# Adding the partial sums of the FFNs' second product into y by an accumulating DMA instead of VectorE

## The chip, the cores and the metric

The kernel runs on one core of a Trainium2 chip. The core has five engines that run side by side, each through its own list of instructions in order: TensorE (PE, matrix products, with its weight loads shown apart as PEld), VectorE (DVE), ScalarE (ACT), GpSimd (POOL) and SyncE (SP, which in this kernel only issues transfers). Matrix products land in PSUM; everything else works in SBUF. The metric is the device time of one execution in microseconds; lower is better.

## The reference, cut to what matters

Two layers of a sequence model over 512 latent and 256 context tokens, each a mixer followed by a SwiGLU FFN of width 2816 on 1024 features. Layer 0's FFN runs on all 768 tokens, layer 1's on the 512 latent ones. The change is inside these two FFNs:

```python
def _swiglu(h, w_gate, w_up, w_down):
    return (jax.nn.silu(h @ w_gate) * (h @ w_up)) @ w_down
...
for l in range(DEPTH):
    ...                                                   # mixer of layer l, out-projection, norms
    h_lat = _modulate(_rms(x_lat, norm_pre_ffn[l]), m_lat[3], m_lat[4])
    x_lat = x_lat + m_lat[5] * _rms(_swiglu(h_lat, ffn_w_gate[l], ffn_w_up[l], ffn_w_down[l]), norm_post_ffn[l])
```

The first product is the pair `h @ w_gate`, `h @ w_up`; the second product is the one with `w_down`. Its sum over the 2816 inner columns is what `y` collects.

## The kernel before, in words

**Numbers.** Every float32 matrix operand is split into a rounded part H and a rest L, and a product is three matmuls (H·H, H·L, L·H). So each weight tile that arrives by DMA (`raw`, 128x1024, a ring of three buffers) is cast by ACT (`wH`, L686 and L741) and subtracted by DVE (`wL`, L687 and L742) before PE can use it. A `raw` buffer comes free when its last cast and subtraction are done, and only then SP, which issues the weight loads in a fixed order, can issue the load that goes into it. L686/L687 are the rows of `w_down`; L741/L742 and the sums `ws`, `raw` (L766) belong to `w_gate` and `w_up`.

**The FFN loop** (function `ffn`) walks the 22 column blocks of 128 two at a time (`c0`). The first two blocks come early (`pearly`). From then on each turn does three things:

- a gate product `go` and an up product `uo`, each by a seven-product scheme on 2x2 blocks (function `seven`; its products have the names 11, U1, 12, U2, 22, S4, V in this order). Product 11, U2 and V use one half of a PSUM tile `ab`, product 12 the other half; E and D are two single PSUM banks. ACT and DVE move each result from PSUM into `go` or `uo`: ACT copies 11 (L805), U1 (L807), U2 (L815), 22 (L817); DVE adds 12 (L813), S4 (L820) and V (L822, L823).
- DVE multiplies `uo` by `go` (L1520); ACT and DVE split the result into `gH`, `gL` (L1522, L1523). `go` and `uo` have one buffer each.
- the second product for the previous pair of blocks (function `acc_part`): for every token tile of 128, PE sums 2 blocks x 3 matmuls for each half of 512 output columns in PSUM (`acc`), and the sum is then added to `y` in SBUF. The tiles take turns in PSUM: one tile takes the two-bank tile `mm` and is added as one 128x1024 piece (a whole), the next takes the two single banks that E and D also use and is added as two 128x512 pieces (halves). The first turn of each layer writes `y` by an ACT copy (L832). All later turns add by DVE (L834). In the last call two blocks are summed together, and each tile goes on to the final norm.

There are ten turns of the loop in each layer; the second product is run for nine of them inside the loop and once after it. Layer 0 has six token tiles, layer 1 four. During layer 0's FFN the kernel also computes modulation vectors in DVE's gaps: DMA loads `mraw`, DVE sums (`macc`, L542, L544).

The program text does not fix the order on each engine. A scheduler arranges all instructions with a cost model of its own, so an edit at one place moves instructions at others. Within an engine the order is then fixed, and an instruction that waits holds all behind it.

Of the kernel before, what the change touches and what calls it, by code (L numbers as in the profile page):

```python
# [8 lines left out]
F32 = mybir.dt.float32  # L9
# [4 lines left out]
ALU = mybir.AluOpType  # L14
# [3 lines left out]
P = 128  # L18
D = 1024
# [311 lines left out]
class Net:  # L331
# [490 lines left out]
                nc.vector.tensor_tensor(c21, c21, pt, op=ALU.subtract)  # L822
                nc.vector.scalar_tensor_tensor(c22, pt, -1.0, c22, op0=ALU.mult, op1=ALU.subtract)  # L823

    def acc_part(self, parts, n, tiles, groups, ys, first, end):


        nc = self.nc

        def add(y, pt):  # L830
            if first:
                nc.scalar.copy(y, pt)  # L832
            else:
                nc.vector.tensor_tensor(y, y, pt, op=ALU.add)  # L834

        for group in groups:
            pts = {}
            for i in group:

                self.whole = not self.whole  # L840
                pt = self.mm_tile("acc") if self.whole else None
                pts[i] = pt, [pt[:, :512], pt[:, 512:]] if self.whole else [self.sc_tile("acc", x) for x in range(2)]
            for p, (units, act) in enumerate(parts):
                done = p == len(parts) - 1
                for i in group:
                    whole, halves = pts[i]
                    t = tiles[i]
                    H, L = (x[:, :, i * P % n : i * P % n + P] for x in act[i * P // n])
                    for hf in range(2):
                        cs = slice(hf * 512, hf * 512 + 512)  # L850
                        for c, unit in enumerate(units):
                            self.mm3(
                                halves[hf],
                                (H[:, c, :], L[:, c, :]),
                                (unit[0][:, 0, cs], unit[1][:, 0, cs]),
                                p == 0 and c == 0,
                                done and c == len(units) - 1,
                            )
                        if done and hf == 0:
                            self.turn(1)  # L860
                        if done and whole is None:
                            add(ys[:, t, cs], halves[hf])
                    if done:
                        if whole is not None:
                            add(ys[:, t, :], whole)
                        end(ys[:, t, :], t)
# [634 lines left out]
    def ffn(self, l, xp, yp, fp, pp, rp, h, ending, extra=None):  # L1501


        nc, I = self.nc, self.I
        wg, wu, wd = I["ffn_w_gate"][l], I["ffn_w_up"][l], I["ffn_w_down"][l]
        tiles, n = h.order, h.n
        extra = extra(fp) if extra else iter(())
        fill = lambda *_: next(extra, None)
        singles = [(i,) for i in range(len(tiles))]

        gp = rp if l else fp

        def gu(x):
            return fp.tile([P, 2, 2 * n], F32, tag=x, bufs=1, name=x)

        def gated(pool, k, g, u, HL=None, mult=True):

            g, u = (x[:, :, n * k : n * k + n] for x in (g, u))
            if mult:
                nc.vector.tensor_tensor(u, u, g, op=ALU.mult)  # L1520
            H, L = HL or h.gated_tiles(pool, k)
            nc.scalar.copy(H, u)  # L1522
            nc.vector.tensor_tensor(L, u, H.bitcast(F32), op=ALU.subtract)  # L1523
            return H, L

        def first():

            cur = h.gated if l else [h.gated_tiles(gp, k) for k in range(2)]
            g, u = gu("go"), gu("uo")
            us = [[self.unit_cols(w, i * P) for w in (wg, wu)] for i in range(2)]  # L1530
            h.open(xp)
            for half in range(2):
                pm = self.mm_tile("pearly")
                pts = [[self.sc_tile("pearly", x)[:, :n] for x in range(2)], [pm[:, 512 * x : 512 * x + n] for x in range(2)]]
                tok = slice(n * half, n * half + n)
                for ks in ((range(4), range(4, 8)) if half == 0 else (range(8),)):
                    for i in range(2):
                        for m in range(2):
                            for k in ks:
                                self.mm3(pts[i][m], tuple(x[:, k, :] for x in us[i][m]), h.raw(k, half), k == 0, k == KD - 1)  # L1540
                            if ks[0] == 0 and half == 0 and m == 0:
                                self.turn(1 - i)
                for i in range(2):
                    nc.scalar.activation(g[:, i, tok], pts[i][0], AF.Silu)
                    nc.vector.tensor_tensor(u[:, i, tok], g[:, i, tok], pts[i][1], op=ALU.mult)
                gated(gp, half, g, u, cur[half], False)
                if half == 0:
                    pp.release()
                    tp = self.open_pool(f"t{l}")
                    h.sums(tp)  # L1550
            h.late()
            return tp, cur

        def units(c0):
            return [self.rows_unit(wd, c0 + i) for i in range(2)]

        def product(w, c0, x, then=None):
            x = gu(x)
            self.seven(self.pair_operands(tp, w, c0 * P, [tp] if l else [], 1 + l), h, x, fill if c0 > 2 else lambda: None, then)
            return x  # L1560

        tp, cur = first()
        y = None
        todo = None
        for c0 in range(2, NFC, 2):
            g = product(wg, c0, "go", todo)
            for k in range(2):
                x = g[:, :, n * k : n * k + n]
                nc.scalar.activation(x, x, AF.Silu)
            if c0 + 2 < NFC:  # L1570
                if y is None:
                    y = yp.tile([P, len(tiles), D], F32, tag="y", bufs=1, name=f"y{l}")
                self.acc_part([(units(c0 - 2), cur)], n, tiles, singles, y, c0 == 2, fill)
                u = product(wu, c0, "uo")
                cur = [h.gated_tiles(gp, k) for k in range(2)]

                def todo(g=g, u=u, cur=cur):
                    for k in range(2):
                        gated(gp, k, g, u, cur[k], True)

            else:
                u = product(wu, c0, "uo")
        for _ in extra:
            pass
        tp.release()
        if gp is not rp:
            rp.release()
        end, follow, pool = ending(y)

        last = [gated(pool, k, g, u) for k in range(2)]  # L1590
        parts = [(units(c0 - 2), cur), (units(c0), last)]
        next(follow, None)
        self.acc_part(parts, n, tiles, [(0, 1)] + singles[2:], y, False, end)
        for left in (2, 1, 0):
            next(follow, None)
            self.turn(left)
        next(follow, None)
        if gp is rp:
            rp.release()
        return y  # L1600
# [232 lines left out]
```

## Time and profile before

| quantity | value |
|---|---|
| time, median of 3 runs | 1762.86 us (1760.73, 1762.86, 1765.64) |
| span of the profiled execution, first to last instruction | 1764.6 us |
| own time of the profiled execution | not given apart from its span |
| mean granted TensorE clock in it | 0.993 |
| PE, DVE, ACT, POOL busy | 1713.0, 1268.5, 865.9, 74.2 us |
| layer 0's FFN loop, steady part | about 480 to 920 us of the span |
| layer 1's FFN loop, steady part | about 1420 to 1740 us of the span |

The span of the profiled execution lies inside the spread of the runs, 1.7 us above their median. In the rows of the profile an instruction group reads: line of the kernel, engine, operation, output and inputs by the program's names, shapes, count, busy time, mean duration in ns, and after the bar the engine's idle time just before these instructions and what ended it. In a list of waits the three numbers are total time, number of waits, and the longest one.

### The profile page before, as it was taken

Reading aid. Unit: us, or ns where it says so; the run is one execution under the profiler, and the core shown is the slowest. Engines: PE = TensorE matmul, PEld = TensorE weight load, DVE = VectorE, ACT = ScalarE, POOL = GpSimd, SP = SyncE. Lnnn points to the kernel's source line nnn. Section 1 sums busy time; section 2 is a strip of 40 time slices with the busy share of each in tenths; the row PEclk is TensorE's granted clock in tenths of the full one; section 3 lists DMA queues with packets and bytes.
Section 4 is the critical chain, followed back from the end, with each engine's and each line's share of the span. In section 5 each row is a group of like instructions: output and inputs, shape, how many; then the busy total and the mean of one; then the engine's idle time right before and its main releaser. Section 6 shows DMA issues by size and latency. Waiting matters only on the chain. (4 is left out here: it accounts for less than half of the span.)

```text
span 1764.6 us, 33117 instructions
## 1 busy us (share of the span) xinstructions
PE 1713.0 (97%) x13888; PEld 1559.9 (88%) x13888; DVE 1268.5 (72%) x2008; ACT 865.9 (49%) x1496; POOL 74.2 (4%) x93
## 2 busy tenths in 40 slices
PE   6999999999999999999999999999999999999998
PEld 3899998988998989889998998888898889998997
DVE  5879646644968999797667418787764678878885
ACT  5545557736543233333346526666654654444343
POOL 1004100001000000000001000000000100000000
PEclk8999999999999999999999999999999999999999
DMA  8731011143434455352225322121124333333333
GB/s 316 225 105 39 2 61 62 49 144 115 136 102 124 146 172 186 113 197 72 72 72 170 104 61 61 50 61 49 50 62 131 120 96 96 96 97 107 98 103 123
DMA packets 169585, 187.26 MB, mean 106 GB/s; under 512 B 6198, under 2 KB 140892, under 8 KB 169436
## 3 DMA queue, kind: packets, MB, share of 16 engines
q1 hardware_dynamic: 167504, 181.56, 32.6%
q10 hardware_dynamic: 1932, 3.59, 0.6%
q8 instruction: 109, 1.79, 0.4%
q14 instruction: 40, 0.33, 0.1%
HBM read 175.66 MB, written 9.46 MB: 105 GB/s over the span
## 5 line engine op out<-in xcount | busy, mean ns | idle before, releaser
L687 DVE TENSOR_TENSOR wL<-raw,wH 128x1024 fp32r<-128x1024 f32 (+1 forms) x126 | 151.2, 1206 | 116.7 <-ACT wH L686 116.4
L362 PE MATMUL nat<-wH,x 128*128 128x256 f32 (+1 forms) x1216 | 227.6, 286 | 0.0
L741 ACT CAST wH<-raw 128x1024 fp32r<-128x1024 f32 x120 | 124.6, 1052 | 176.6 <-PE acc L362 73.4
L362 PEld LDWEIGHTS nat<-wH,x 128*128 128x128 f32 x1216 | 192.4, 192 | 2.3 <-ACT natq L1098 0.8
L742 DVE TENSOR_TENSOR wL<-raw,wH 128x1024 fp32r<-128x1024 f32 x120 | 145.2, 1220 | 64.3 <-ACT wH L741 64.2
L686 ACT CAST wH<-raw 128x1024 fp32r<-128x1024 f32 (+1 forms) x126 | 128.9, 1038 | 116.6 <-PE nat L362 34.2
L362 PE MATMUL nat<-wL,x 128*128 128x256 f32 (+1 forms) x608 | 173.0, 285 | 0.0
L362 PE MATMUL acc<-wH,gH 128*128 128x512 f32 x440 | 172.6, 393 | 0.0
L362 PE MATMUL acc<-wH,gL 128*128 128x512 f32 x440 | 171.7, 390 | 0.0
L362 PE MATMUL acc<-wL,gH 128*128 128x512 f32 x440 | 171.5, 390 | 0.0
L834 DVE TENSOR_TENSOR y<-y,acc 128x1024 f32<-128x1024 f32 x135 | 114.8, 862 | 31.3 <-PE acc L362 28.0
L362 PE MATMUL ff<-x,wH 128*128 128x512 f32 (+1 forms) x512 | 127.6, 340 | 0.0
L544 DVE SCALAR_TENSOR_TENSOR macc<-mraw,scT,macc 128x1024 f32<-128x1024 f32 x98 | 122.6, 1276 | 6.3 <-DMA mraw<-in_mod_w_dram 6.3
L614 POOL TENSOR_TENSOR rs<-ms,neghalf 128x1 f32<-128x1 f32 (+2 forms) x62 | 58.2, 939 | 1612.6 <-DVE ms L612 1606.4
L362 PEld LDWEIGHTS nat<-wL,x 128*128 128x128 f32 x608 | 116.9, 192 | 0.1
L362 PE MATMUL oproj<-wH,x 128*128 128x512 f32 x320 | 102.0, 396 | 3.4 <-ACT x L1248 3.4
L362 PEld LDWEIGHTS acc<-wH,gH 128*128 128x128 f32 x440 | 82.6, 188 | 19.7 <-issue 1.7
L362 PEld LDWEIGHTS acc<-wH,gL 128*128 128x128 f32 x440 | 82.6, 188 | 17.3
L362 PEld LDWEIGHTS acc<-wL,gH 128*128 128x128 f32 x440 | 82.7, 188 | 16.2
L362 PEld LDWEIGHTS ff<-x,wH 128*128 128x128 f32 x512 | 87.3, 190 | 10.0
L937 ACT COPY qkh<-arr 128x512 f32<-128x512 f32 x112 | 70.2, 643 | 36.6 <-DVE arr L942 32.4
L362 PE MATMUL ff<-x,wL 128*128 128x256 f32 (+1 forms) x256 | 86.2, 337 | 0.0
(345 smaller groups left out, 4102.9 us busy)
## 6 DMA issues: line engine op xcount, KB each, us to landing
mraw<-in_mod_w_dram SPq DMA_DIRECT2D x96, 512.0 KB, 4.7
raw<-in_ffn_w_gate_dram SPq DMA_DIRECT2D x44, 512.0 KB, 3.8
raw<-in_ffn_w_up_dram SPq DMA_DIRECT2D x44, 512.0 KB, 4.0
raw<-in_ffn_w_down_dram SPq DMA_DIRECT2D x44, 512.0 KB, 3.6
raw<-in_odd_w_in_dram SPq DMA_DIRECT2D x40, 512.0 KB, 4.0
raw<-in_even_w_in_dram SPq DMA_DIRECT2D x16, 512.0 KB, 4.2
x<-xr SPq DMA_DIRECT2D x14, 512.0 KB, 2.7
xr<-x SPq DMA_DIRECT2D x14, 512.0 KB, 3.4
```

The lines of the kernel that those rows point to most:

```text
L362: return self.pin(self.nc.tensor.matmul(*a, **k))
L544: nc.vector.scalar_tensor_tensor(a, u, w, a, op0=ALU.mult, op1=ALU.add)
L614: nc.gpsimd.tensor_tensor(rs, ms, self.neghalf.to_broadcast([P, w]), op=ALU.pow)
L686: nc.scalar.copy(H[:, :m], raw[:, :m])
L687: nc.vector.tensor_tensor(L[:, :m], raw[:, :m], H[:, :m].bitcast(F32), op=ALU.subtract)
L741: self.nc.scalar.copy(H, f)
L742: self.nc.vector.tensor_tensor(L, f, H.bitcast(F32), op=ALU.subtract)
L834: nc.vector.tensor_tensor(y, y, pt, op=ALU.add)
L937: nc.scalar.copy(qkv[:, :, :, half, :], dst)
```

## The change: what it does

`acc_part` gets a function `by_dma`. Where that function gives a buffer (`ypart`), ACT copies the partial sum from PSUM to the buffer, and a DMA issued on POOL's queue adds the buffer to `y` in SBUF. In layer 1 every partial sum of the loop after the first turn goes this way, wholes and halves, with four buffers; in layer 0 only the halves do, with two buffers, and the wholes stay with DVE. The last call, after the loop, stays with DVE in both layers.

```diff
-    def acc_part(self, parts, n, tiles, groups, ys, first, end):
+    def acc_part(self, parts, n, tiles, groups, ys, first, end, by_dma=None):
         nc = self.nc
         def add(y, pt):
             if first:
                 nc.scalar.copy(y, pt)
+            elif by_dma is not None and (s := by_dma(pt.shape[-1])) is not None:
+                nc.scalar.copy(s, pt)
+                nc.gpsimd.dma_start(out=y, in_=s, accum_op=ALU.add)
             else:
                 nc.vector.tensor_tensor(y, y, pt, op=ALU.add)
...
+        def part(m):
+            if l:
+                return fp.tile([P, D], F32, tag="ypart", bufs=4, name="ypart")[:, :m]
+            return fp.tile([P, m], F32, tag="ypart", bufs=2, name="ypart") if m == 512 else None
...
-                self.acc_part([(units(c0 - 2), cur)], n, tiles, singles, y, c0 == 2, fill)
+                self.acc_part([(units(c0 - 2), cur)], n, tiles, singles, y, c0 == 2, fill, part)
```

Line numbers from the inserted lines on shift by 3, and behind `part` by 8 (L1520 becomes L1528, L1523 becomes L1531, L1569 becomes L1577).

The scheduler's new order differs at three places of each turn of layer 1. First ACT, from the Silu of `go` (L1569, now L1577) over the second product to the first copy of the next up product. Before:

```order
L1569 ACTIVATE go<-go 128x2x256 x2
L741 CAST dH<-ws 128x512
L741 CAST wH<-raw 128x1024 x2
L805 COPY uo<-ab 128x256
L807 COPY uo<-E 128x256
```

Now:

```order
L1577 ACTIVATE go<-go 128x2x256 x2
L834 COPY ypart<-acc 128x1024
L741 CAST dH<-ws 128x512
L834 COPY ypart<-acc 128x512 x2
L834 COPY ypart<-acc 128x1024
L834 COPY ypart<-acc 128x512
L741 CAST wH<-raw 128x1024
L834 COPY ypart<-acc 128x512
L741 CAST wH<-raw 128x1024
L805 COPY uo<-ab 128x256
```

Of the two casts that stood together, the second now stands behind the copy of the last half.

Second PE, at the start of the gate product that follows (E is product U1, D is product 22, `ab<-x` is product 12). Before:

```order
L362 MATMUL E<-T_14925,wH 128x256 x2
L362 MATMUL E<-T_14925,wL 128x256
L362 MATMUL D<-x_14765,wH 128x256 x2
L362 MATMUL ab<-x_14764,wH 128x256 x2
L362 MATMUL ab<-x_14764,wL 128x256
```

Now:

```order
L362 MATMUL E<-T_15021,wH 128x256 x2
L362 MATMUL E<-T_15021,wL 128x256
L362 MATMUL ab<-x_14860,wH 128x256 x2
L362 MATMUL ab<-x_14860,wL 128x256
L362 MATMUL ab<-x_14860,wH 128x256 x2
```

Two matmuls of product 22 that stood ahead of product 12 now stand behind it.

Third DVE, from the end of the up product into the gate product (`ws` is the first sum on a newly loaded pair of up weights). Before:

```order
L687 TENSOR_TENSOR wL<-raw,wH 128x1024
L822 TENSOR_TENSOR uo<-uo,ab 128x256
L823 SCALAR_TENSOR_TENSOR uo<-ab,uo 128x256
L1520 TENSOR_TENSOR uo<-uo,go 128x2x256 x2
L687 TENSOR_TENSOR wL<-raw,wH 128x1024
L1523 TENSOR_TENSOR gL<-uo,gH 128x512 x2
L813 TENSOR_TENSOR go<-go,ab 128x256
L766 TENSOR_TENSOR ws<-raw 128x512
```

Now:

```order
L687 TENSOR_TENSOR wL<-raw,wH 128x1024
L822 TENSOR_TENSOR uo<-uo,ab 128x256
L823 SCALAR_TENSOR_TENSOR uo<-ab,uo 128x256
L1528 TENSOR_TENSOR uo<-uo,go 128x2x256 x2
L687 TENSOR_TENSOR wL<-raw,wH 128x1024
L766 TENSOR_TENSOR ws<-raw 128x512
L1531 TENSOR_TENSOR gL<-uo,gH 128x512 x2
L813 TENSOR_TENSOR go<-go,ab 128x256
```

`ws` has moved ahead of the split (L1523, now L1531) and of the addition of product 12 (L813).

## The prediction

> **What bounds the kernel now.** First the busy shares, over the span and over the steady part of each FFN (columns there: stretch, its length, then busy time and count of PE, PEld, DVE, ACT, POOL, granted clock, share of the DMA engines, GB/s).
>
> ```profile
> span 1764.6 us, 33117 instructions
> ...
> PE 1713.0 (97%) x13888; PEld 1559.9 (88%) x13888; DVE 1268.5 (72%) x2008; ACT 865.9 (49%) x1496; POOL 74.2 (4%) x93
> ```
>
> ```profile
> 480.00:920.00 440.00, 433.16 (x2275) 395.80 (x2274) 360.74 (x449) 155.01 (x215) 0.00 (x0) 1.00 0.41 127
> 1420.00:1740.00 320.00, 312.98 (x2159) 290.60 (x2159) 250.13 (x351) 146.22 (x228) 0.00 (x0) 1.00 0.34 103
> ```
>
> PE is the bound: in layer 0's FFN it lacks 6.8 us of 440, in layer 1's 7.0 of 320. So freeing DVE can give back some 14 us at the most, and only where DVE's lateness is what PE waits for. POOL is empty in both, so its queue delays no older work. Next PE's waits, layer 0 (480 to 920) and then layer 1 (1420 to 1740):
>
> ```profile
> PE ab L362 <- DVE uo L813: 3.9, 3, 2.1
> PE ab L362 <- ACT go L805: 1.9, 2, 1.4
> ...
> PE ab L362 <- DVE go L813: 1.0, 2, 0.6
> ```
>
> ```profile
> PE ab L362 <- ACT go L805: 5.0, 9, 1.2
> ```
>
> None is a wait for `acc`'s PSUM to be emptied by the additions (L834). In layer 1 one wait comes back in every turn: product 12 of the gate product waits for ACT's copy of product 11 (L805). The chain of work that ended last shows what makes that copy late (start, length, what):
>
> ```profile
> 1563.70 10.92 PE acc L362 x48
> ...
> 1574.64 0.69 DVE y L834
> 1575.33 2.28 DVE wL L742 x2
> ...
> 1577.63 5.20 DMA raw<-in_ffn_w_up_dram
> ...
> 1582.85 1.06 ACT wH L741
> ...
> 1585.49 1.14 DVE wL L687
> ...
> 1587.80 0.70 DVE uo L1520
> ...
> 1589.03 1.69 PE ab L362 x12
> 1590.72 1.08 PE D L362 x9
> ```
>
> When `acc` ends, DVE adds the last half, makes two `wL`, and with the second a `raw` buffer comes free. Only then can SP issue the next up load. ACT's cast and DVE's `wL` wait for it, and in DVE's order the additions to `uo` and the multiplication L1520 stand behind this `wL`; L1520 frees `go`, ACT copies, PE goes on:
>
> ```profile
> 1583.93 1.23 DVE L742 TENSOR_TENSOR wL<-raw,wH 128x1024 fp32r<-128x1024 f32 x1 [4.48 <-ACT wH L741]
> 1589.03 0.50 PE L362 MATMUL ab<-x,wH 128*128 128x256 f32 x2 [0.98 <-ACT go L805]
> ```
>
> So the 32 us turn already has no slack on this path: whatever delays that load delays PE by as much.
>
> **What the change removes.** The additions by DVE, in layer 0 and in layer 1:
>
> ```profile
> L834 DVE TENSOR_TENSOR y<-y,acc 128x512 f32<-128x512 f32 x48 | 32.5, 683 | 5.8 <-PE acc L362 4.3
> ```
>
> ```profile
> L834 DVE TENSOR_TENSOR y<-y,acc 128x512 f32<-128x512 f32 x32 | 21.9, 686 | 5.6 <-PE acc L362 3.9
> L834 DVE TENSOR_TENSOR y<-y,acc 128x1024 f32<-128x1024 f32 x16 | 19.5, 1217 | 0.2 <-PE acc L362 0.2
> ```
>
> That is 32.5 + 21.9 + 19.5 = 74 us of DVE. In layer 1 it is worth nothing directly: in the chain only the last half (0.69 us) is on the path, and something else takes its place (below). In layer 0 it is worth part of PE's 6.8 us. But the two largest of those waits stand behind a load of modulation weights, not behind additions; DVE idled for it just ahead of L813:
>
> ```profile
> 652.61 1.28 DVE L544 SCALAR_TENSOR_TENSOR macc<-mraw,scT,macc 128x1024 f32<-128x1024 f32 x1 [1.78 <-DMA mraw<-in_mod_w_dram]
> ```
>
> ```profile
> 753.10 1.28 DVE L544 SCALAR_TENSOR_TENSOR macc<-mraw,scT,macc 128x1024 f32<-128x1024 f32 x1 [2.30 <-DMA mraw<-in_mod_w_dram]
> ```
>
> Less DVE work does not bring these loads forward. I leave out about half of the 6.8, and set against the remaining 3.4 some 1.4 for new traffic beside the `mraw` loads: layer 0 gives **-2**, with bounds -6.8 (every wait gone) and +4.1 (DVE's two waits here, 1.78 + 2.30, once more).
>
> **What it adds on ACT.** 80 halves and 16 wholes, priced by the copies of the first turn, which read the same PSUM tile (minimum, median, maximum in ns; the maximum is a whole):
>
> ```profile
> L832 ACT COPY y<-acc x15: 578/591/1018, 489.8 to 1446.4; 128x512 f32<-128x512 f32 x10, 128x1024 f32<-128x1024 f32 x5
> ```
>
> 80 x 0.59 + 16 x 1.02 = 63.5 us. ACT is 35% to 46% busy in the two stretches, so the sum is hidden; the order is not. In layer 1 the last half and the two casts behind `acc` now go copy, cast, copy, cast, with the tile ends read from the chain's 48 matmuls (0.2275 us each): the fifth partial sum is ready at 1573.3 and copied by 1573.9, the first cast runs 1574.0 to 1575.05, the last copy (its sum ready at 1574.6) to 1575.65, the second cast to 1576.65. Before, the casts ended at 1576.01:
>
> ```profile
> 1574.01 2.00 ACT L741 CAST wH<-raw 128x1024 fp32r<-128x1024 f32 x2 [4.16 <-PE acc L362]
> ```
>
> DVE's second `wL` then ends at about 1576.65 + 1.2 = 1577.85 in place of 1577.61: the load is issued **0.25 us later**. Removing DVE's last addition buys nothing, since ACT's copy stands in its place.
>
> **What the new order moves.** PE: two matmuls of 0.12 us (nine took 1.08) that filled time ahead of the wait now stand behind it: **+0.24 us**. DVE: `ws` now stands ahead of L1523 and L813, and needs the second up load.
>
> ```profile
> 1577.63 9.40 SPq L763 DMA_DIRECT2D raw<-in_ffn_w_up_dram  x2
> ```
>
> ```profile
> 1588.40 1.22 DVE L687 TENSOR_TENSOR wL<-raw,wH 128x1024 fp32r<-128x1024 f32 x1
> ...
> 1591.01 0.41 DVE L813 TENSOR_TENSOR go<-go,ab 128x256 f32<-128x256 f32 x1
> ```
>
> ```profile
> raw<-in_ffn_w_gate_dram SPq DMA_DIRECT2D x18, 512.0 KB, 3.7
> raw<-in_ffn_w_up_dram SPq DMA_DIRECT2D x20, 512.0 KB, 4.0
> ```
>
> The second load is issued at about 1586.7 (0.38 us before the row's end) and lands 3.7 us later, at 1590.4 (the median of its neighbour, since the up median of 4.0 includes the crowded first one). `ws` (0.69) ends at 1591.1, L1523 (two, 1.2) at 1592.3, L813 at 1592.7. PE, with products 12, 22 and three matmuls of S4 in between (27 x 0.12 = 3.24 from 1589.03), is ready for U2 at 1592.3: **+0.35 us**. Together the order costs 0.25 + 0.24 + 0.35 = 0.84 us in each of the eight turns that add by DMA; below, these could overlap with each other and cost 0.25.
>
> **What it adds on the queues.** POOL issues 48 + 32 halves (256 KB) and 16 wholes (512 KB), 29 MB, 2.1 MB in each turn of layer 1. No trace shows an accumulating transfer or one issued on POOL, so it is bounded. The nearest row is the weight queue in layer 1 (packets, MB, share of 16 engines):
>
> ```profile
> q1 hardware_dynamic: 42832, 31.99, 33.5%
> ```
>
> 33.5% of 320 us for 32 MB is 3.35 us of all engines per MB. In front of and beside the critical load stand the last three partial sums (a whole copied by 1573.0, halves by 1573.9 and 1575.65), 1.05 MB: 3.5 us if the bytes move once, 7 if reading `y` counts as well. SP's two loads there (a `w_down` load and the critical one) also take 3.5 us. Lower bound of the delay: 0, if the sums have drained first. Upper bound: 3.5 us, if the two queues share the engines evenly all the while. I take **1.5**, near the 1.76 us of the two halves moved once, as the whole is likely gone by 1577.6. [...]
>
> Waits that the buffers add: layer 1's fifth copy (1573.3) needs the first sum (copied by 1567.5) landed, 5.8 us; layer 0's third half needs the first, two tiles or 24 matmuls later: 5.46 - 0.59 = 4.9 us. Against loads of 3.7 to 4.0 us this costs nothing; it comes back as a rival. An addition into the same piece of `y` is a turn of 32 us away, and the tail's additions stay with DVE: nothing there.
>
> **Sum.** Layer 1: 8 x (0.84 + 1.5) = +18.7. Layer 0: -2. Against the profiled span of 1764.6 this gives 1781.3; that span stands 1.7 above the median of the runs, so I forecast **1779**, slower by 0.9%.
>
> **The rivals.**
> - The transfers are hidden: the sums drain before the critical load, and the delay is 0. Then 8 x 0.84 = 6.7, layer 0 -3.4: 1766, no measurable change. For it: the DMA engines are busy only 34% of the time. Against: the load goes out within 2 us of the last copy.
> - Faster: DVE's relief in layer 0 takes away all of PE's 6.8 us, as its `mraw` sums are done sooner, the loads go out sooner and L813 is no longer late: 1756. It decides if layer 1 loses less than 1.5 us in all, that is if the load is no later than now. For it: DVE at 82% is layer 0's busiest helper. Against: the two rows on `mraw` above.
> - Much slower: an accumulating transfer of 512 KB takes longer than 5.8 us. Then ACT waits at its fifth copy with the casts behind it. At 9 us: 3.2 for the buffer, 3.5 for shared engines, 0.84: 7.5 x 8 = 60, so 1823. Against: it needs more than double a load's time. [...]
>
> **How the numbers follow.** Forecast 0.50, hidden 0.22, faster 0.15, much slower 0.13. Two runs of this kernel differ by about 0.3% (5.3 us), so that is what counts as no change. Faster takes the third case, 0.15; same the second with a little of the forecast's low edge, 0.23; slower 0.62. The forecast's own range is 1765 (delay 0.3, overlapped order costs: 8 x 0.55 - 2 = 2.4) to 1802 (delay 3.5, layer 0 at its upper bound: 8 x 4.34 + 4.1 = 38.8). The range of 1757 to 1803 adds the hidden case and nearly all the way to the faster one, and leaves out the much slower one and half of the faster.
>
> **What would show it.** In layer 1 the up load behind `acc` lands more than 5.2 us after its issue, PE's waits on L805 grow from 5.0 us to about 20, L813 of `go` appears among PE's waits, and turns lengthen from 32 to some 34.5 us. In layer 0 PE's waits stay above 3 us. ACT gains 64 us, DVE loses 74. Wrong it is if the load lands as now (then 1766 or less), or if ACT's idle time names POOL's transfers (then well above 1803).

## The result: slower by 2.8%, and the profile after

The changed kernel takes 1811.4 us (median of 4 runs, 1810.1 to 1816.9) against 1764.0 us (4 runs, 1760.7 to 1765.6). The ratio is 1.0281 with a 95% interval of 1.0264 to 1.0298. I had forecast 1779 us with a range of 1757 to 1803: the direction was right, the size was not. The loss is 47.5 us where the sum had 16.7.

First, lines of the page after: span, busy time, DMA queues (packets, MB, share of 16 engines). In the new kernel's numbering the copies stand in L834, the new DMAs in L835, VectorE's remaining additions in L837, and what was L1520, L1523 and L1569 is now L1528, L1531 and L1577.

```profile
span 1810.9 us, 33344 instructions
...
PE 1731.2 (96%) x13888; PEld 1574.0 (87%) x13888; DVE 1203.9 (66%) x1912; ACT 923.7 (51%) x1592; POOL 157.4 (9%) x189
...
q1 hardware_dynamic: 167504, 181.56, 31.7%
q0 software_dynamic: 13824, 29.37, 9.8%
```

ACT has 58 us more and DVE 65 us less, much as announced (the rows of neighbouring instructions overlap by some 0.1 us, so 74 us of rows are 65 of busy time). PE does the same 13888 matmuls in 18 us more, so some of them ran slower. The new queue q0 moved 29.37 MB in 9.8% of the engines' time: 0.098 x 1810.9 / 29.37 = **6.0 us of all engines per MB**, where the weight queue q1 has 0.317 x 1810.9 / 181.56 = 3.2. These shares add up the times of packets (the pieces a transfer is cut into), so "engine time" here means packet time; where packets overlap, the share of a short stretch passes 1 (1.05 below, that is 16.8 packets at once on the mean).

The two FFN stretches after (length, busy time and count of PE, PEld, DVE, ACT, POOL, granted clock, DMA share, GB/s):

```profile
480.00:920.00 440.00, 428.80 (x2234) 390.12 (x2233) 329.33 (x394) 176.89 (x255) 41.91 (x48) 0.99 0.58 153
1420.00:1740.00 320.00, 293.80 (x1925) 271.40 (x1925) 196.19 (x277) 162.40 (x251) 38.46 (x45) 0.95 0.58 136
```

In layer 1 PE now lacks 26 us of 320 (7.0 before), and its granted clock fell from 1.00 to 0.95. The waits there (1425 to 1760; total, times, longest) after:

```profile
ACT wH L741 <- DMA raw<-in_ffn_w_up_dram: 30.4, 9, 5.6
...
PE E L362 <- DVE uo L820: 17.1, 8, 3.5
...
PE ab L362 <- ACT go L805: 9.3, 7, 1.8
...
ACT ypart L834 <- DMA y<-ypart: 0.3, 1, 0.3
```

The first row was 7.3 us in 9 waits in the same window of before. The second is new. It is the same path as in the prediction, met one step earlier: the gate product's second product, U1, writes bank E, and DVE must empty E first (L820). L820 stands in DVE's queue behind the `wL` that waits for the late up load. One turn of the chain of waits after:

```profile
1704.70 0.58 ACT ypart L834
1705.28 0.96 ACT wH L741
...
1706.27 1.24 DVE wL L742
1707.52 9.44 DMA raw<-in_ffn_w_up_dram
...
1716.98 1.05 ACT wH L741
...
1719.20 0.41 DVE uo L820
...
1722.70 0.38 ACT go L805
...
1723.13 2.93 PE ab L362 x12
```

The load takes 9.4 us where the same step took 5.2. The last row shows a second cost: 12 matmuls in 2.93 us, 1.69 before. They come behind PE's longest wait there (the timeline's row of the first U1 product, its wait in brackets):

```profile
1719.67 0.80 PE L362 MATMUL E<-T,wH 128*128 128x256 f32 x2 [3.52 <-DVE uo L820]
```

Why the load is late can be read in the stretches around its issue, and why the matmuls are slow in the stretch after the stall. First before, the 6 us from the load's issue; then after, the 7 us ahead of the issue at 1707.5 (`acc` ends at 1704.4), the 6 us from it, and 6 us after the stall (columns as above):

```profile
1577.00:1583.00 6.00, 6.00 (x50) 5.81 (x50) 1.02 (x2) 0.90 (x3) 0.00 (x0) 1.00 0.64 179
```

```profile
1700.00:1707.00 7.00, 7.00 (x44) 6.26 (x43) 1.96 (x2) 4.35 (x6) 3.32 (x4) 1.00 1.05 189
```

```profile
1707.00:1713.00 6.00, 6.00 (x51) 5.81 (x50) 0.91 (x2) 0.75 (x2) 0.00 (x0) 1.00 1.03 211
```

```profile
1723.00:1729.00 6.00, 5.87 (x27) 5.88 (x28) 4.78 (x8) 2.35 (x7) 0.00 (x0) 0.50 0.45 132
```

The 16 DMA engines are full (1.03; 0.64 before) when the critical load is issued, and they already were in the 7 us ahead of it (1.05). After the stall PE's granted clock is 0.50. The transfers themselves (KB each, median us from issue to landing):

```profile
y<-ypart POOLq DMA_DIRECT2D x80, 256.0 KB, 5.4
...
y<-ypart POOLq DMA_DIRECT2D x16, 512.0 KB, 5.2
```

In layer 0 (480 to 920) the waits after are these; the `macc` row was 6.3 us in 6 waits before, and PE's 3.9:

```profile
ACT ypart L834 <- DMA y<-ypart: 21.4, 8, 7.1
DVE macc L544 <- DMA mraw<-in_mod_w_dram: 18.0, 16, 2.7
PE ab L362 <- DVE uo L813: 6.9, 4, 2.1
```

Where the 46.3 us between the two profiled spans (1764.6 and 1810.9) went, from the starts of the first and last `acc` of each layer in the trace: layer 0 446.0 to 453.2 us (+7.2); between the layers +0.2; layer 1 301.9 to 338.7 (+36.9); before the first `acc` -0.4, behind the last +2.5.

### The profile page after: what moved, and what is told of

Its sections match the earlier page's. It is cut to its first block, busy times and chain, and to the rows that moved or that the text cites. A ratio compares the mean times of both kernels' runs of the same rounds, so it can differ in the third digit from the quotient of the medians.

```text
span 1810.9 us, 33344 instructions
## 1 busy us (share of the span) xinstructions
PE 1731.2 (96%) x13888; PEld 1574.0 (87%) x13888; DVE 1203.9 (66%) x1912; ACT 923.7 (51%) x1592; POOL 157.4 (9%) x189
## 3 DMA queue, kind: packets, MB, share of 16 engines
q1 hardware_dynamic: 167504, 181.56, 31.7%
q0 software_dynamic: 13824, 29.37, 9.8%
## 5 line engine op out<-in xcount | busy, mean ns | idle before, releaser
L687 DVE TENSOR_TENSOR wL<-raw,wH 128x1024 fp32r<-128x1024 f32 (+1 forms) x126 | 151.1, 1205 | 117.3 <-ACT wH L686 116.9
L835 POOL DMA_DIRECT2D y<-ypart x96 | 83.3, 875 | 704.7 <-ACT ypart L834 610.4
L834 ACT COPY ypart<-acc 128x512 f32<-128x512 f32 (+1 forms) x96 | 63.1, 658 | 124.3 <-PE acc L362 100.2
L362 PE MATMUL E<-T,wH 128*128 128x384 f32 (+1 forms) x320 | 73.8, 320 | 17.5 <-DVE uo L820 17.1
```

The source lines that it names most:

```text
L362: return self.pin(self.nc.tensor.matmul(*a, **k))
L687: nc.vector.tensor_tensor(L[:, :m], raw[:, :m], H[:, :m].bitcast(F32), op=ALU.subtract)
L834: nc.scalar.copy(s, pt)
L835: nc.gpsimd.dma_start(out=y, in_=s, accum_op=ALU.add)
```

## The experiments

Theory: the accumulating transfers cost about twice a load's engine time per byte (6.0 against 3.2 us per MB); those in flight when the up load behind `acc` is issued delay it; PE stalls, and restarts at a lower clock (0.50 in the stretch above). Rivals: the new order of instructions (ACT's copies between the casts) costs it, not the transfers; every transfer costs a fixed price; ACT waits for its `ypart` buffers; bytes cost the same wherever they stand in the turn.

All experiments are edits of the changed kernel. "Turn" is the mean time between `acc` starts over turns two to eight of layer 1 in the profiled run, "load" the range of the up loads behind `acc` that the chain shows in those turns, "layer 0" the time from its first to its last `acc`. Each ratio is to runs of the kernel before on the same chip (medians of 1760.9 to 1764.0 us).

| kernel | median us | ratio to before (95%) | turn | load | layer 0 |
|---|---|---|---|---|---|
| before | 1764.0 | | 32.4 | 4.4 to 5.5 | 446.0 |
| changed | 1811.4 | 1.0281 (1.0264 to 1.0298) | 37.3 | 6.8 to 9.4 | 453.2 |
| layer 1 alone | 1801.3 | 1.0227 (1.0210 to 1.0244) | 36.8 | 6.8 to 8.9 | 442.1 |
| layer 0 alone | 1771.1 | 1.0047 (1.0026 to 1.0068) | 32.4 | 4.6 to 5.0 | 449.0 |
| copies, then DVE adds | 1766.7 | 1.0024 (1.0013 to 1.0035) | 32.9 | 4.1 to 4.6 | 442.8 |
| plain writes | 1773.3 | 1.0070 (1.0050 to 1.0091) | 32.9 | 4.4 to 5.4 | 448.9 |
| layer 1, 64 columns | 1767.6 | 1.0042 (1.0027 to 1.0057) | 32.9 | 4.5 to 5.3 | 443.1 |
| copies only | 1763.1 | 1.0014 (1.0004 to 1.0023) | 32.9 | 4.4 to 5.1 | 438.1 |
| layer 1, first three sums | 1761.8 | 1.0005 (0.9996 to 1.0015) | 32.4 | 4.3 to 5.2 | 443.7 |
| layer 1, last three sums | 1792.2 | 1.0183 (1.0168 to 1.0198) | 36.0 | 6.9 to 8.7 | 442.4 |
| layer 1, half the columns | 1773.0 | 1.0072 (1.0058 to 1.0086) | 33.6 | 5.0 to 6.1 | 442.0 |
| layer 1, five buffers | 1798.2 | 1.0204 (1.0187 to 1.0221) | 37.4 | 7.5 to 9.1 | 442.1 |
| layer 0, 64 columns | 1761.5 | 1.0006 (0.9997 to 1.0015) | 32.5 | 4.6 to 5.7 | 441.4 |
| layer 0, GpSimd adds | 1765.0 | 1.0029 (1.0018 to 1.0040) | 32.3 | 4.6 to 5.2 | 447.7 |

Layer 0 scatters by itself: in kernels that leave it as before it takes 442.0 to 443.7 us, so the 446.0 of the profiled run of before is at its long end.

**One layer at a time.**

```diff
-y, c0 == 2, fill, part)
+y, c0 == 2, fill, part if l else None)     # layer 1 alone
+y, c0 == 2, fill, None if l else part)     # layer 0 alone
```

> Only layer 1 adds by DMA; layer 0 adds with VectorE as before. Theory (the accumulating transfers share the DMA engines with the up load that PE waits for, at about twice a load's engine time per byte, and ACT waits for its ypart buffers): the loss of layer 1 stays whole, about 37 us in its loop and 2 behind it, so 1800 to 1806, and layer 0 comes back to its time of before. Rival (the two layers' losses share a cause, such as POOL's work or a lower clock over the whole kernel): it falls by more than the 7 us that layer 0 shows, to 1795 or less.

> Only layer 0 adds by DMA; layer 1 adds with VectorE as before. Theory: layer 0's 7 us alone, 1768 to 1774. My term in the prediction said -2: 1762. Rival (common cause over the whole kernel): 1780 or more.

Layer 1 alone costs 40 us (0.0227 x 1761), layer 0 alone 8 (1.0047). They add up to the whole (47.5), so a common cause is out. My -2 for layer 0 had the wrong sign.

**The order without the transfers.** ACT copies as in the change, VectorE adds from SBUF.

```diff
 nc.scalar.copy(s, pt)
-nc.gpsimd.dma_start(out=y, in_=s, accum_op=ALU.add)
+nc.vector.tensor_tensor(y, y, s, op=ALU.add)
```

> ScalarE copies each partial sum to ypart as in the change, but VectorE adds it from there: the same copies on ACT, no accumulating DMA. Theory (the DMAs are the cost): only the order's part stays, 8 turns of 0.25 to 0.84 us and up to 0.7 us each for VectorE's addition that now stands behind ACT's last copy: 1766 to 1777. Rival (ACT's copies standing between the casts are the cost): 1795 or more, with DVE waiting for ACT's cast without a late load.

Turns of 32.9 us: the order costs 0.4 us each, and 4 us in all. The rest of layer 1's loss is the transfers'.

**The same transfers without the addition.**

```diff
-nc.gpsimd.dma_start(out=y, in_=s, accum_op=ALU.add)
+nc.gpsimd.dma_start(out=y, in_=s)
```

> The same transfers from POOL's queue without the addition (y is overwritten, so the additions are left out of what is computed). Theory (an accumulated byte costs about twice the engine time of a loaded one, and lands later for it): about half of the 46 us goes, 1780 to 1792, and the queue's share of the engines falls from 9.8% to about 5%. Rival 1 (it is the queue or POOL's way of issuing, whatever the transfer does): 1805 to 1815. Rival 2 (only the read and write of y at the destination is slow): below 1772.

```profile
q0 software_dynamic: 8704, 29.37, 4.5%
...
y<-ypart POOLq DMA_DIRECT2D x80, 256.0 KB, 2.6
y<-ypart POOLq DMA_DIRECT2D x16, 512.0 KB, 3.2
```

The same 29.37 MB take 0.045 x 1777.4 / 29.37 = 2.7 us per MB, less than half of the accumulating 6.0, and land in half the time. More went away than the theory expected (1773 against 1780 to 1792), and the time lies next to the second rival's bound of 1772: in layer 1 the turn is that of the copies alone, so its price goes with the addition. In the 6 us from the load's issue the engines are not full:

```profile
1582.00:1588.00 6.00, 6.00 (x50) 5.81 (x50) 1.35 (x2) 1.07 (x3) 0.00 (x0) 1.00 0.72 221
```

So the delay does not go in proportion to the transfers' whole engine time: it is there when the engines are full at that moment, and otherwise hardly. That POOL issues, and how often, costs layer 1 nothing that this run shows. Layer 0, though, is as slow as with additions (448.9 against 449.0).

**Few bytes.** Layer 1 alone, 64 columns of each piece; the other columns are not added.

```diff
-nc.gpsimd.dma_start(out=y, in_=s, accum_op=ALU.add)
+nc.gpsimd.dma_start(out=y[:, :64], in_=s[:, :64], accum_op=ALU.add)
```

> Layer 1 alone by DMA, and each of its transfers accumulates only the first 64 columns of its piece (the other columns are not added): the same 48 issues on POOL, an eighth of the bytes of a half and a sixteenth of a whole's. Theory (engine time goes with the accumulated bytes, and it is this that delays the critical up load): that load lands in 4.4 to 5.5 us again, turns of 32.9 us as with the copies alone, 1764 to 1771. Rival (each accumulating transfer has a fixed price, whatever its size): 1793 or more.

Again 32.9 us: a fixed price for each accumulating transfer is out.

**Nothing added at all.** Only the copy stays.

```diff
 nc.scalar.copy(s, pt)
-nc.gpsimd.dma_start(out=y, in_=s, accum_op=ALU.add)
```

> ScalarE copies the partial sums, and nobody adds them (this part of the sum is left out): VectorE is relieved of 74 us and there is no transfer. Theory: the relief is worth nothing in layer 1, since the copies stand in the place of the additions (turns of 32.9 us as in the run with copies and VectorE's additions, 0.6 above before), and at most 5 us in layer 0: 1759 to 1768. Rival (VectorE's relief is worth what PE waits for it, and the transfers took it back): below 1757. Rival for layer 0 (its 5 to 7 us come from the instructions' new order, which brings VectorE to the modulation sums before their loads, and not from transfers): first to last acc of layer 0 in 448 us or more, and a total above 1768.

This is the most that the change could have brought: 1763.1, not faster than before, though DVE is relieved of 66 us. With these copies layer 1's turn is 32.9 whether VectorE adds or not. In layer 0 the relief is real (438.1 against 442 to 444), and layer 1's copies take it back.

**Where in the turn.** Layer 1 alone; half of its sums by DMA, the others by VectorE.

```diff
-elif by_dma is not None and (s := by_dma(pt.shape[-1])) is not None:
+elif by_dma is not None and (s := by_dma(pt.shape[-1], group[0])) is not None:
...
-def part(m):
+def part(m, i):
+    if i > 1:              # first three sums; i < 2 for the last three
+        return None
```

> Layer 1 alone, and only the first two of its four tiles (a whole and two halves, 1.05 MB of the 2.1 MB in a turn) by DMA; the last two tiles are added by VectorE as before. Theory (the accumulating transfers still in flight when the up load behind acc is issued delay it): they drain during the second half of acc, so the load lands in 4.4 to 5.5 us and the order behind acc is that of before: turns of 32 to 32.7 us, 1758 to 1768. Rival (every accumulated byte costs the same wherever it stands): half of the 40 us, 1778 to 1784.

> The other half: layer 1 alone, only its last two tiles by DMA, the first two by VectorE. The same bytes. Theory: these are the ones in flight, so most of the loss stays: load 6 to 8.5 us, turns of 35 to 36.5 us, 1784 to 1797. Rival (every accumulated byte costs the same wherever it stands): 1778 to 1784, and the same as the first three.

These two settle it. The same 8.39 MB cost nothing early in `acc` (1.0005) and 32 us late in it (1.0183). The chain's up load and the 6 us from its issue, first three sums:

```profile
1576.39 5.04 DMA raw<-in_ffn_w_up_dram
```

```profile
1576.00:1582.00 6.00, 6.00 (x50) 5.81 (x50) 0.78 (x2) 1.29 (x3) 0.00 (x0) 1.00 0.57 179
```

Last three sums:

```profile
1583.54 8.72 DMA raw<-in_ffn_w_up_dram
```

```profile
1583.00:1589.00 6.00, 6.00 (x51) 5.81 (x50) 0.93 (x2) 0.74 (x2) 0.00 (x0) 1.00 1.04 222
```

**Half the bytes, spread over all sums.** Layer 1 alone.

```diff
+m = pt.shape[-1] // 2
-nc.gpsimd.dma_start(out=y, in_=s, accum_op=ALU.add)
+nc.gpsimd.dma_start(out=y[:, :m], in_=s[:, :m], accum_op=ALU.add)
```

> Layer 1 alone, and each transfer accumulates only the first half of its columns (the other half is not added): 1.05 MB in a turn, spread over all six sums, so that the last three hold about as much engine time (0.5 MB at 6 us per MB, 3.1 us) as the plain writes' last three did (2.8 us). Theory (what counts is the engine time in flight when the up load is issued): load 4.4 to 6 us, turns of 32.9 to 34 us, 1765 to 1775. Rival (an accumulating transfer blocks the loads beside it for other reasons than its engine time): load 6.5 us or more and turns of 35 us or more, 1781 or more.

```profile
1576.07 6.07 DMA raw<-in_ffn_w_up_dram
```

```profile
1576.00:1582.00 6.00, 6.00 (x50) 5.81 (x49) 0.46 (x2) 0.60 (x2) 0.00 (x0) 1.00 0.69 187
```

As many accumulated bytes as in the last two runs, and 12 us, of which the copies alone explain 5 to 7: the engines are 0.69 busy, and the loads take 5.4 us on the mean (4.9 before). So in these runs an accumulating transfer did not block by itself; the delay came with the engine time in flight, as the next table shows (0.8 us of it here, 3.4 to 3.8 where the load is late).

The DMA packets in the traces give that time directly. Between the issue and the landing of the up load behind `acc`, the packets of POOL's queue take the following engine time (mean over the loads that the chain shows in turns two to eight):

| kernel | engine time of POOL's queue beside the load, us | the load, us |
|---|---|---|
| before | 0 | 4.9 |
| layer 1, first three sums | 0 | 4.8 |
| plain writes | 0.1 | 4.8 |
| layer 1, 64 columns | 0.4 | 4.8 |
| layer 1, half the columns | 0.8 | 5.4 |
| layer 1, last three sums | 3.4 | 7.4 |
| layer 1 alone | 3.8 | 8.0 |

Where much is left to move when the load is issued, the load is longer by most of it (3.1 of 3.8 us, 2.5 of 3.4). The plain writes cost layer 1 so little because their last packet ends 0.2 us after the issue, and the first three sums because theirs ended 1.5 to 2.6 us ahead of it.

**More buffers.**

```diff
-tag="ypart", bufs=4
+tag="ypart", bufs=5          # layer 1 alone
```

> Layer 1 alone as in the first experiment, with five ypart buffers in place of four: the fifth copy no longer needs the first sum landed (my much slower rival's wait). Theory (the load behind acc is late because of the engines' time, the buffers' wait costs 0.3 us in all): no change, 1796 to 1805. Rival (ACT's wait for a buffer is part of it): 1790 or less.

No change (1.0204 against 1.0227). The wait for a buffer, from my rival "much slower", plays no part in layer 1.

**Layer 0: the bytes, and another way to relieve VectorE.** The first run has the 64 columns of above in layer 0 alone, the second lets GpSimd add.

```diff
-nc.gpsimd.dma_start(out=y, in_=s, accum_op=ALU.add)
+nc.gpsimd.tensor_tensor(y, y, s, op=ALU.add)     # layer 0 alone
```

> Layer 0 alone, and each transfer accumulates only the first 64 columns of its half (the rest is not added). Theory (layer 0's 10 us come from the bytes, which share the engines with the loads of modulation weights that VectorE waits for; 13.6 to 18 us of such waits with whole transfers, plain or accumulating, 5.4 without any): the waits fall back to 5 to 8 us, first to last acc to 438 to 443 us, total 1757 to 1765. Rival (the order of the instructions or the issues on POOL cost it): first to last acc 447 us or more, 1768 or more.

> Layer 0 alone: ScalarE copies each half to ypart as in the change, and GpSimd adds it to y itself, with no transfer; layer 1 as before. It is the relief of VectorE without bytes on the DMA engines. Theory: first to last acc 438 to 442 us as with copies alone, total 1753 to 1761, at best 0.4% faster than before. Rival (GpSimd's addition takes longer than the 4.9 us that a ypart buffer has, or slows VectorE beside it): ACT waits for ypart, 1766 or more.

With few bytes layer 0's loss is gone (1.0006), and DVE's wait for modulation weights falls from 15.3 us (layer 0 alone, whole transfers) to 7.9:

```profile
DVE macc L544 <- DMA mraw<-in_mod_w_dram: 15.3, 17, 2.4
```

```profile
DVE macc L544 <- DMA mraw<-in_mod_w_dram: 7.9, 14, 1.1
```

So layer 0's loss, too, comes with the bytes. GpSimd's additions missed what I expected: 447.7 us and 1.0029. ACT never waits for `ypart` there; the other half of the rival fits, as VectorE's own instructions got longer, though no run shows that this is what the 5 us are. First before, then with GpSimd adding (480 to 920, busy and mean ns):

```profile
L544 DVE SCALAR_TENSOR_TENSOR macc<-mraw,scT,macc 128x1024 f32<-128x1024 f32 x64 | 80.4, 1278 | 6.3 <-DMA mraw<-in_mod_w_dram 6.3
L742 DVE TENSOR_TENSOR wL<-raw,wH 128x1024 fp32r<-128x1024 f32 x57 | 69.1, 1220 | 33.6 <-ACT wH L741 33.6
L766 DVE TENSOR_TENSOR raw<-raw 128x512 f32<-128x512 f32 x57 | 39.1, 686 | 0.6
```

```profile
L544 DVE SCALAR_TENSOR_TENSOR macc<-mraw,scT,macc 128x1024 f32<-128x1024 f32 x64 | 86.9, 1382 | 4.7 <-DMA mraw<-in_mod_w_dram 4.6
L742 DVE TENSOR_TENSOR wL<-raw,wH 128x1024 fp32r<-128x1024 f32 x57 | 73.7, 1299 | 39.6 <-ACT wH L741 39.3
L766 DVE TENSOR_TENSOR raw<-raw 128x512 f32<-128x512 f32 x57 | 47.7, 837 | 1.0
```

None of the variants beats the kernel before; the best full one is level with it.

## Why the prediction was wrong

**The step that failed is the delay of the critical load.** I had 1.5 us per turn, "near the 1.76 us of the two halves moved once, as the whole is likely gone by 1577.6". Both parts were wrong. A byte that is accumulated costs 6.0 us of all engines per MB, so the last three sums (1.05 MB) hold 6.3 us, near the 7 that I had given for the case that reading `y` counts as well and then set aside. And the whole was not gone: the six sums of a turn take 2.1 x 6.0 = 12.6 us of all engines and arrive within the 11 us of `acc`, beside the weight loads, so the engines are full (1.05) before the load goes out, and 3.8 us of engine time are still to come (layer 1 alone). The prediction asked what lies in front of the load; it should also have asked whether the queue drains at all during `acc`. Loads of 4.9 us (mean of six turns of before in the chain) became 8.0 (mean of five, layer 1 alone): +3.1, inside my upper bound of 3.5. Put into my sum with the measured order (0.4) and layer 0 (+8), this delay gives 1763 + 28 + 8 = 1799, still in the range.

**A term that was missing is the clock,** and it takes this estimate to 1808, past the range. Behind the wait of 3.52 us above PE's matmuls ran slower (12 in 2.93 us, 1.69 before), at a granted clock of 0.50. In layer 1 alone PE's busy time for the same matmuls grew by 8.7 us (1713.0 to 1721.7), 1.1 us for each of eight turns, and its granted clock over layer 1's loop (1420 to 1740) is 0.96, where before has 1.00. The profiled run is the fastest of its four, with a mean clock of 0.987 against 0.983 and 0.984 in the others, so the term may be larger in them. What is left up to 1811, some 4 us, fits turns that are 0.5 us longer in the changed kernel than in layer 1 alone.

| per turn of layer 1 | predicted | measured |
|---|---|---|
| order of copies, matmuls, `ws` | 0.84 | 0.4 (copies without transfers) |
| delay of the up load | 1.5 | 3.1 |
| slower matmuls behind the stall | 0 | about 1.1 |
| sum | 2.3 | 4.6; turns 4.4 longer |

The clock's term rests on busy time and the granted clock alone; no run kept the stall and removed the slow clock.

**Layer 0 had the wrong sign.** I gave -2 for relief and took the price of traffic from two waits doubled. The relief was there (first to last `acc` 438 us with copies only), but DVE's waits for `mraw` went from 6.3 us to 18.0, more than the 4.1 I had added as the bound, and layer 0 alone lost 8 us in the medians. What stays open is why plain writes, with less than half the engine time, cost layer 0 as much as accumulating ones. One profile of each and a scatter of 2 to 4 us in that layer don't tell.

**What was right.** The path: load, cast, `wL`, DVE's queue, PE, in each turn. The order's cost lay inside its bounds of 0.25 to 0.84. POOL's issues and ACT's 63 us are hidden, and freeing DVE in layer 1 is worth nothing (copies only: the same turn of 32.9 us as with DVE's additions). The `ypart` waits cost nothing in layer 1 (five buffers). In layer 0 ACT waits 21.4 us for them, but with plain writes, where 1.5 us of them are left, the layer takes as long; that is one profile of each, and not a proof. There I had named the wrong sign to look for, "if ACT's idle time names POOL's transfers (then well above 1803)": it did, and in layer 1 it was not the cause. L805's waits did not grow to 20 us, because L820 in the same queue waits first; the two together have 26.4. L813 of `go` hardly shows there (0.4 us).

**The rivals.** Hidden: it is what the first three sums alone show, 1.0005. Faster: its 6.8 us of relief did not show against 442 to 444 us (copies only gained 4 to 6), and traffic took more. Much slower: a median landing of 5.2 us is under the 5.8 it needed, and five buffers changed nothing. That the time came near it is chance: it came by another way.

In the changed kernel the packets of the two queues ran side by side behind `acc` (issue at 1707.5): POOL's go on to 1715.1, and the first one of the weight queue comes at 1709.55, 2.0 us after the late load's issue and 3.5 us after that of the `w_down` load ahead of it (before: 1.0 us after the issue of that `w_down` load).

## What to carry to other kernels

An accumulating DMA is paid in engine time, here more than twice that of a plain write (6.0 against 2.7 us per MB), so count its bytes against the engines' free time in the stretch where it runs, not against the mean share (34% before, and yet full, at 1.03, at the one moment that mattered). Put it where the engines can drain before the next load that someone waits for: early in the stretch it cost nothing, late it cost 32 us with the same bytes. And relieving an engine is worth nothing where the work taken off it is not what the critical path waits for; leaving the additions out altogether shows the most it could bring, before anything is built.

## What the hardware showed that I had not expected

- Accumulating from SBUF to SBUF took 6.0 us of all 16 engines per MB, plain writes of the same bytes 2.7. With rows of 256 bytes it was dearer still: 1.1% of 1767.7 us for 1.58 MB, 12 us per MB.
- POOL's issue of an accumulating transfer took 0.86 us or more (96 of them 83.3 us), of a plain one 0.54 (52.2 us).
- After a wait of 3.52 us PE's granted clock was 0.50 over the 6 us from 1723, where before layer 1 holds 1.00. In layer 1 alone it was 0.50 as well after one of 2.48 us (the row behind the wait, then the 3 us from there):

```profile
1485.91 0.80 PE L362 MATMUL E<-T,wH 128*128 128x256 f32 x2 [2.48 <-DVE uo L820]
```

```profile
1486.00:1489.00 3.00, 2.85 (x12) 2.55 (x12) 3.00 (x6) 0.48 (x2) 0.00 (x0) 0.50 0.22 63
```

In another turn of layer 1 alone, behind a wait of 2.95 us, pairs of matmuls took 0.63 us, against 0.40 ahead of it; with five buffers, behind a wait of 3.22 us, they took 0.40 from the second pair on. So these runs show no length of wait from which on the clock falls.
- With GpSimd's additions (1.63 us for a half) the three VectorE instructions shown above took 6% to 22% longer on the mean, while the addition L820 of `go` kept its 547 ns, and the two-operand instructions L687, L1528 and L1531 their 1218, 950 and 951. What sets the longer ones apart is not shown.
